# Norm chains with n-wide operands in PSUM, S5 copies of both steps at once, and an order chosen with slack and drawn durations

## The chip, the cores and the metric

The kernel runs on one core of one Trainium2 chip. The core has TensorE (PE, matrix products; PEld is its weight load), VectorE (DVE), ScalarE (ACT), GpSimd (POOL) and SyncE (SP, which issues the DMAs). The metric is the device time of one execution in microseconds (us). Before the change it is 1505.81 us, the median of three runs (1504.4 to 1506.77).

## The reference

It computes two transformer blocks in float32 on 512 tokens of width 1024. Block 1 is an RMS norm, a projection to an attention mixer of three branches (compressed, selected, windowed) and a retention mixer, an output projection, a second RMS norm and a squared-ReLU FFN of width 4096. Block 2 is modulated by a conditioning vector (adaLN): a standardized input goes through a hybrid mixer of an mLSTM (4 heads) and an S5 state space model (32 groups of 16 channels, 64 states), then through a gated FFN with a short convolution, each followed by a layer norm of the scaled residual. What the change touches, cut to the core:

```python
def rms_norm(x, w):
    y = x * lax.rsqrt(jnp.mean(x * x, axis=-1, keepdims=True) + EPS)
    return y * w

def _standardize(x):
    mu = jnp.mean(x, axis=-1, keepdims=True)
    var = jnp.mean(jnp.square(x - mu), axis=-1, keepdims=True)
    return (x - mu) * lax.rsqrt(var + LN_EPS)

# mLSTM, one chunk: numerator, normalizer and the norm of each head
h = num / jnp.maximum(jnp.abs(den), jnp.exp(-m_t))[..., None]
hm = _standardize(hm)

# S5: a diagonal complex recurrence per group, then the output map
_, _, xr, xi = lax.associative_scan(combine, (a_r, a_i, bu_r, bu_i), axis=1)
y = jnp.einsum('gcp,bsgp->bsgc', c_re, xr) - jnp.einsum('gcp,bsgp->bsgc', c_im, xi)
ys = jax.nn.gelu(y + d * u)
```

## The kernel before, in words

All activations lie with channels on the 128 partitions and the 512 tokens along the row. Every large product is a sum of three matmuls: weights and activations are split into a high and a low part (`w`/`xsh`/`xsl`, `wkh`/`wkl` and the like), accumulated in a PSUM bank `ps_g`. Weights arrive by DMA as `wraw`; ACT makes the high part, DVE the low one. PE works on these products nearly all the time, and the norms, the attention, the mLSTM and S5 are threaded into that stream.

The order is not the order of the source. The class `Order` (from line 176) records every instruction with its operands; `add` finds dependences by comparing regions, where `region` (218) takes any PSUM access for the whole bank. `time` (249), `shares` (290) and `latency` (303) are a model of durations, of the port that DVE and POOL share, and of hand-over times. `flush` (311) tries several priorities, plays each through `simulate` (381), which issues per engine what is ready and looks `AHEAD` = 800 instructions ahead, and keeps the order whose modelled end is earliest. `issue` (515) then emits the instructions in that order, so nearly every row of the profile has line 519, and instructions are told apart by their tiles. The order is final: each engine works its own list from first to last, waiting at its head.

The norms need 1/sqrt. `newton` (702) computes it on DVE without a table: a first guess `y` from the bits of `v`, half of `-v` in `a`, three rounds of Newton's method. For up to four columns (one per 128 tokens) each step is done one column at a time, 128x1, with the column as a per-partition scalar. The tile names carry the caller's prefix: `r1`, `rk`, `rq`, `r3` (RMS and retention norms; `r3v`, `r3a`, `r3t`, `r3y`), `rm` (the mLSTM's norm; its inputs `md`, `me`, its result applied to `nm`), `rl` (standardization). The result `..y` is broadcast over the partitions by a PE transpose (`ps_t<-cf,rly`, where `cf` is the identity), which is where PE can wait for DVE.

`standardize` (1315) is used twice, in two halves of 256 tokens each: `add_up` (1306) sums the eight tiles `x` of the residual into two tiles `lsum` (on POOL and DVE in turn) and their squares `sq` (ACT) likewise, for k = 2 to 5; `token_means` (738) then adds the two sums and the tiles of k = 6 and 7 over the channels by tiny matmuls (`ps_s<-lsum,mean`, `ps_s<-x,mean`, `ps_s<-sq,mean`), copies the result (`tm`) and transposes it. `standardize2` (1402) standardizes twice in a row (the output of block 1 and the input of block 2 in one) from six sums per token in `wa`: `wm` and `wv` are its second mean and variance, `wm`, `wa` and `rly` are transposed by PE.

The end of the kernel is the last product of the FFN (`ps_g<-fmh,wkh` ...), whose eight output tiles go in two halves of tokens through `standardize`, then `pair` (product with the factor, then gain and bias on ACT or DVE), then to DRAM. The first half's `pair` work runs beside the second half's matmuls, the second half's behind them.

`s5_out` (2183) makes S5's output in four quarters of groups. Per quarter: 8 matmuls `ps_o<-U,s5k` on the input, and 8 matmuls `ps_o<-s5z,wraw` on the states `X`, which DVE first copies into `s5z`, a tile that is zeroed by POOL and filled by 32 copies of 64 partitions x 32 numbers. Then ACT copies the result to `y5`, and after a way through DRAM a gelu follows. The mLSTM runs beside it (`qkh`, `W`, `Wh`, `nm`; its gate `om` is made by ACT with a bias `gb` that DVE computes).

Of the kernel before, what the change touches and what calls it, by code (L numbers as in the profile page):

```python
# [20 lines left out]
S = 512  # L21
D = 1024
SLOTS = 70
AHEAD = 800
# [151 lines left out]
class Order:  # L176
# [40 lines left out]
    @staticmethod  # L217
    def region(ap, t):

        if t.psum:  # L220
            return 0, 128, 0, 1
        dims, o = [(int(s), int(c)) for s, c in ap.ap], int(ap.offset)
        p0, pc = 0, 1
        if not t.dram:
            (ps, pc), dims = dims[0], dims[1:]
            p0, o = divmod(o, ps)
        lo = o + sum(s * (c - 1) for s, c in dims if s < 0)
        hi = o + sum(s * (c - 1) for s, c in dims if s > 0)
        return p0, p0 + pc, lo, hi + 1

    def add(self, engine, fn, args, kw):
        i, deps, use = len(self.ops), set(), {}
        for a, w in [(a, n == 0) for n, a in enumerate(args)] + [(a, k == "accum_out") for k, a in kw.items()]:
# [4 lines left out]
            r, keep = self.region(a, t), []  # L238
# [10 lines left out]
    def time(self, engine, fn, args, kw):  # L249
# [5 lines left out]
        cols = sum(self.width(a) == 1 for a in aps[1:]) if wide > 1 else 0  # L255
# [9 lines left out]
        if engine == "vector":  # L265
            return 68 + wide * (6.25 if fn == "reciprocal" else 1.042) + 61 * cols + 60 * ("accum_out" in kw)
# [23 lines left out]
    def shares(self, op):  # L290

        aps = [a for a in [*op.args[1:], *op.kw.values()] if hasattr(a, "tensor")]
        if op.engine == "gpsimd":
            return len(aps) > 0
        if op.engine != "vector" or any(a.tensor.name in self.psum for a in [op.args[0], *aps]):
            return False
        one = self.width(op.args[0]) == 1
        return op.fn in ("tensor_tensor", "scalar_tensor_tensor") or op.fn in ("tensor_scalar", "tensor_copy") and not one
# [12 lines left out]
    def flush(self):  # L311
# [11 lines left out]

        best, early, late = None, [0.0] * N, self.latest()
# [56 lines left out]
    def simulate(self, prio, early, alike=0, apart=150.0):  # L381
# [19 lines left out]
        parked, order, events, over = {}, [], [], {}  # L401
        issued, later, low = [op.engine == "sync" for op in ops], [], 0
# [27 lines left out]
        while len(order) < N:  # L430
            now, e = min(((st.free[e] if ready[e] else max(st.free[e], avail[e][0][0]), e)
                          for e in self.ENGINES if ready[e] or avail[e]), default=(math.inf, None))
            if events and events[0][0] <= now:
                time, name = heapq.heappop(events)
                st.live[tiles[name].key].discard(name)
                wake(tiles[name].key, time)
# [23 lines left out]
            else:  # L460
                start[i] = now
                for name in new:
                    wake(tiles[name].key, now)
                if e == "sync":
# [3 lines left out]
                    st.dma = max(now + hold + 650.0, st.dma, lane) + op.time  # L468
# [44 lines left out]
        return SimpleNamespace(order=order, start=start, end=max(fin))  # L513
# [8 lines left out]
class Kern:  # L522
# [167 lines left out]
    def rsqrt(self, ssum, n, scale, eps, name, post=None, bufs=2):  # L690

        v = self.small(name + "v", n, bufs)
# [9 lines left out]
    def newton(self, v, n, name, post=None, bufs=2):  # L702

        V = self.nc.vector
        y, a, t = (self.small(name + c, n, bufs) for c in "yat")
        if n <= 4:

            y_, a_, t_, v_ = ([x[:, j:j + 1] for j in range(n)] for x in (y, a, t, v))
            for j in range(n):
                V.tensor_scalar(y_[j].bitcast(I32), v_[j].bitcast(I32), -0.5, float(0x5F3759DF), op0=OP.mult, op1=OP.add)  # L710
                V.tensor_scalar(a_[j], v_[j], -0.5, None, op0=OP.mult)
            for i in range(3):
                for j in range(n):
# [3 lines left out]
            if post:  # L717
                for j in range(n):
                    V.tensor_scalar(y_[j], y_[j], post, None, op0=OP.mult)
            return y  # L720
        V.tensor_scalar(y.bitcast(I32), v.bitcast(I32), -0.5, float(0x5F3759DF), op0=OP.mult, op1=OP.add)
        V.tensor_scalar(a, v, -0.5, None, op0=OP.mult)
        for _ in range(3):
            V.tensor_tensor(t, y, y, op=OP.mult)
            V.tensor_tensor(t, t, a, op=OP.mult)
            V.scalar_tensor_tensor(y, t, 1.5, y, op0=OP.add, op1=OP.mult)
        if post:
            V.tensor_scalar(y, y, post, None, op0=OP.mult)
        return y
# [8 lines left out]
    def token_means(self, groups):  # L738
# [9 lines left out]
        T.transpose(pt[:, 0:128], t, self.ident)  # L748
        return pt[:, 0:128].rearrange("p (q r) -> p q r", r=32)[:, :, 0]
# [169 lines left out]
    def head_factors(self, st, name):  # L919

        V, A, T = self.nc.vector, self.nc.scalar, self.nc.tensor
        n = st.n

# [209 lines left out]
    def attention(self):  # L1133
# [3 lines left out]
        den = self.const.tile([128, 4, 2, 2, 4], F32, name="den")  # L1137
# [4 lines left out]
        def scores(r, br, i, P):  # L1142
# [6 lines left out]
            for g in range(2):  # L1149
# [9 lines left out]
                A.activation(P[g][:, o], ps[:, 0:n], AF.Exp, bias=mx, accum_out=den[:, i, br, g, r:r + 1])  # L1159
            d = den[:, i, br, :, r]  # L1160
# [145 lines left out]
    def add_up(self, sums, x, k, c):  # L1306
        s, q = sums
        e = (self.nc.gpsimd, self.nc.vector)[k % 2]
        if 1 < k < 6:
            e.tensor_tensor(s[k % 2][:, c], (x[k - 2] if k < 4 else s[k % 2])[:, c], x[k][:, c], op=OP.add)  # L1310
        self.nc.scalar.activation(q[k][:, c], x[k][:, c], AF.Square)
        if 1 < k < 6:
            e.tensor_tensor(q[k % 2][:, c], q[k % 2][:, c], q[k][:, c], op=OP.add)

    def standardize(self, x, hf, sums, each, eps=1e-5):
# [6 lines left out]
        pv = self.token_means([[u[:, tok[j]] for u in t] for t in ([*s, *x[6:]], [*q[0:2], *q[6:]]) for j in range(2)])  # L1322
        m, w, v = (self.small("l" + n, 2, 2) for n in "mwv")
        V.tensor_copy(m, pv[:, 0:2])
        V.scalar_tensor_tensor(w, pv[:, 0:2], -1.0, m, op0=OP.mult, op1=OP.mult)
        if isinstance(eps, float):
            V.scalar_tensor_tensor(v, pv[:, 2:4], eps, w, op0=OP.add, op1=OP.add)
        else:
            V.tensor_tensor(v, pv[:, 2:4], w, op=OP.add)
            for j in range(2):  # L1330
                V.tensor_scalar(v[:, j:j + 1], v[:, j:j + 1], eps[:, 2 * hf + j:2 * hf + j + 1], None, op0=OP.add)
# [70 lines left out]
    def standardize2(self, x, hf, st, gain, bias, each):  # L1402
# [8 lines left out]
        a = self.small("wa", 12, 2).rearrange("p (n j) -> p n j", j=2)  # L1411
        V.tensor_copy(a, pv[:, 0:12].rearrange("p (j n) -> p n j", j=2))
        m, s1, s2, s3, q, q2 = (a[:, n] for n in range(6))
        c1, c2, c3, c4 = (st.cs[:, n:n + 1] for n in range(4))
        v = self.small("wv", 2, 2)
        each_ = lambda *vs: [[u[:, j:j + 1] for u in vs] for j in range(2)]
        for m_, v_, q_ in each_(m, v, q):
            V.tensor_scalar(v_, m_, m_, -1.0, op0=OP.mult, op1=OP.mult)
        for m_, v_, q_ in each_(m, v, q):
            V.tensor_scalar(v_, v_, 1e-5, q_, op0=OP.add, op1=OP.add)  # L1420
# [3 lines left out]
        r = self.newton(v, 2, "rl")  # L1424

        for m_, a1, a2, a3, p_ in each_(m, s1, s2, s3, q2):
            V.tensor_scalar(a1, m_, c1, a1, op0=OP.mult, op1=OP.subtract)
            V.tensor_scalar(a3, m_, c3, a3, op0=OP.mult, op1=OP.subtract)
            V.tensor_scalar(a2, m_, c2, a2, op0=OP.mult, op1=OP.subtract)
            V.tensor_scalar(p_, a2, m_, p_, op0=OP.mult, op1=OP.add)  # L1430
            V.tensor_scalar(p_, a1, a1, p_, op0=OP.mult, op1=OP.subtract)
# [7 lines left out]
        m2, v2 = self.small("wm", 2, 2), self.small("wv", 2, 2)  # L1439
        for v_, p_, r_, a3 in each_(v2, q2, r, s3):  # L1440
            V.tensor_scalar(v_, p_, r_, a3, op0=OP.mult, op1=OP.add)
        for v_, r_ in each_(v2, r):
# [888 lines left out]
```

## Time and profile before

| | |
|---|---|
| median of three runs | 1505.81 us (1504.4 to 1506.77) |
| the profiled execution: its own time | 1505.45 us |
| its span | 1503.3 us |
| granted TensorE clock, mean | 0.991 |
| PE busy | 1461.9 us (97%) |
| DVE / ACT / POOL busy | 1124.8 / 688.6 / 569.8 us |
| on the chain that ended last | PE 86%, DVE 10%, DMA 2%, ACT 1% |

The span runs from the first to the last instruction of the execution; its own time is 2.2 us longer. Busy time of the helpers says little here: with PE busy for 97% of the span, what matters is the few places in which PE is not. Those are read from its waits (what released PE after idling), from the timeline around them, and from the granted clock in windows, since PE can work at less than full clock after it has stood still. Most matmuls show as two records, and ends overlap the next start, so the step from start to start is the time that a matmul costs.

### The profile page before, as it was taken

Reading aid. Unit: us, or ns where it says so; the run is one execution under the profiler, and the core shown is the slowest. Engines: PE = TensorE matmul, PEld = TensorE weight load, DVE = VectorE, ACT = ScalarE, POOL = GpSimd, SP = SyncE. Lnnn points to the kernel's source line nnn. Section 1 sums busy time; section 2 is a strip of 40 time slices with the busy share of each in tenths; the row PEclk is TensorE's granted clock in tenths of the full one; section 3 lists DMA queues with packets and bytes.
Section 4 is the critical chain, followed back from the end, with each engine's and each line's share of the span. In section 5 each row is a group of like instructions: output and inputs, shape, how many; then the busy total and the mean of one; then the engine's idle time right before and its main releaser. Section 6 shows DMA issues by size and latency. Waiting matters only on the chain.

```text
span 1503.3 us, 24351 instructions
## 1 busy us (share of the span) xinstructions
PE 1461.9 (97%) x8738; PEld 1221.4 (81%) x8738; DVE 1124.8 (75%) x2641; ACT 688.6 (46%) x1397; POOL 569.8 (38%) x583
## 2 busy tenths in 40 slices
PE   9999999999999999999999899999999999999996
PEld 6779656888888777899778777878888899998996
DVE  6896798998974674565887863656488999897886
ACT  6454465444333333453563354434265555454553
POOL 6332334240060660143186102120127357464635
PEclk9999999999999999999999899999999999999998
DMA  6731114858731533415313543345311133323331
GB/s 218 224 108 64 56 43 160 267 193 279 235 116 42 176 129 119 153 46 176 107 57 100 158 137 124 119 147 180 143 63 51 50 106 99 116 88 106 100 97 57
DMA packets 81065, 188.34 MB, mean 125 GB/s; under 512 B 18352, under 2 KB 28528, under 8 KB 80944
## 3 DMA queue, kind: packets, MB, share of 16 engines
q1 hardware_dynamic: 80944, 186.78, 38.5%
q8 instruction: 69, 1.13, 0.3%
q14 instruction: 52, 0.43, 0.1%
HBM read 168.70 MB, written 15.17 MB: 122 GB/s over the span
## 4 chain that ended last, share of the span: by engine, by line
PE 86%; DVE 10%; DMA 2%; ACT 1%; issue 1%; POOL 0%; SPq 0%; ACTq 0%; DVEq 0%; POOLq 0%
PE ps_g L519 72%; PE ps_s L519 6%; PE ps_o L519 5%; PE ps_t L519 3%; DVE s5z L519 1%; DVE w L519 1%; DVE x L519 1%; DVE rlt L519 1%; DMA wraw<-in_w_fg_dram 1%; DVE rly L519 0%; DVE r3t L519 0%; DVE rmt L519 0%; DMA wraw<-in_w_f_dram 0%; DVE r3y L519 0%; DMA wraw<-in_w_down_dram 0%
## 5 line engine op out<-in xcount | busy, mean ns | idle before, releaser
L519 DVE TENSOR_TENSOR w<-wraw,w 128x512 fp32r<-128x512 f32 (+2 forms) x390 | 321.3, 837 | 92.2 <-ACT w L519 87.8
L519 ACT ACTIVATE w<-wraw 128x512 fp32r<-128x512 f32 (+1 forms) x398 | 240.3, 609 | 318.0 <-PE ps_g L519 248.6
L519 PE MATMUL ps_g<-xsh,w 128*128 128x256 f32 (+1 forms) x1088 | 278.8, 338 | 2.6 <-DVE w L519 2.2
L519 PE MATMUL ps_g<-xh,w 128*128 128x512 f32 x736 | 240.2, 398 | 0.0
L519 PEld LDWEIGHTS ps_g<-xsh,w 128*128 128x128 f32 x1088 | 188.6, 190 | 28.7 <-DVE w L519 2.6
L519 PE MATMUL ps_g<-xsl,w 128*128 128x256 f32 (+1 forms) x544 | 182.6, 336 | 0.0
L519 PEld LDWEIGHTS ps_g<-xh,w 128*128 128x128 f32 x736 | 137.7, 188 | 33.6 <-issue 1.9
L519 PE MATMUL ps_g<-xl,w 128*128 128x512 f32 x368 | 145.9, 397 | 0.0
L519 PE MATMUL ps_g<-mdh,w 128*128 128x512 f32 (+1 forms) x480 | 143.7, 374 | 0.1
L519 POOL TENSOR_TENSOR x<-x,lc 128x256 f32<-128x256 f32 x72 | 52.6, 773 | 185.9 <-ACT lc L519 173.7
L519 PEld LDWEIGHTS ps_g<-xsl,w 128*128 128x128 f32 x544 | 103.3, 190 | 11.0
L519 PE MATMUL ps_g<-tfh,w 128*128 128x256 f32 x576 | 107.5, 281 | 0.9 <-DVE wo L519 0.4
L519 PEld LDWEIGHTS ps_g<-mdh,w 128*128 128x128 f32 x480 | 87.1, 188 | 17.9 <-issue 0.8
L519 PE MATMUL ps_g<-fmh,w 128*128 128x512 f32 (+1 forms) x332 | 101.4, 375 | 0.0
L519 PEld LDWEIGHTS ps_g<-tfh,w 128*128 128x128 f32 x576 | 89.7, 188 | 2.1 <-DVE wo L519 0.9
L519 PE MATMUL ps_g<-mdl,w 128*128 128x512 f32 (+1 forms) x240 | 89.6, 373 | 0.0
L519 PEld LDWEIGHTS ps_g<-xl,w 128*128 128x128 f32 x368 | 69.2, 188 | 15.6
L519 PE MATMUL ps_g<-tfl,w 128*128 128x256 f32 x288 | 78.0, 281 | 0.0
L519 POOL TENSOR_TENSOR ws<-wraw 128x512 f32<-128x512 f32 x36 | 57.1, 1591 | 51.7 <-DMA wraw<-in_w_fv_dram 27.2
L519 DVE SCALAR_TENSOR_TENSOR raw<-raw,silu 128x1024 f32<-128x1024 f32 x48 | 62.7, 1305 | 9.7 <-DMA raw<-in_w_ada_dram 9.2
L519 PEld LDWEIGHTS ps_g<-fmh,w 128*128 128x128 f32 x332 | 59.8, 188 | 10.3 <-issue 0.2
L519 DVE TENSOR_TENSOR w<-ws,w 128x512 fp32r<-128x512 f32 x72 | 58.7, 829 | 11.1 <-ACT w L519 10.8
(510 smaller groups left out, 3471.1 us busy)
## 6 DMA issues: line engine op xcount, KB each, us to landing
raw<-in_w_ada_dram SPq DMA_DIRECT2D x48, 512.0 KB, 4.3
wraw<-in_w_dram SPq DMA_DIRECT2D x36, 512.0 KB, 3.7
wraw<-in_w_up_dram SPq DMA_DIRECT2D x32, 512.0 KB, 4.2
wraw<-in_w_down_dram SPq DMA_DIRECT2D x32, 512.0 KB, 3.7
wraw<-in_w_fv_dram SPq DMA_DIRECT2D x22, 512.0 KB, 3.9
wraw<-in_w_fg_dram SPq DMA_DIRECT2D x22, 512.0 KB, 3.7
wraw<-in_w_f_dram SPq DMA_DIRECT2D x14, 512.0 KB, 4.3
wraw<-in_w_fd_dram SPq DMA_DIRECT2D x16, 384.0 KB, 3.1
```

What stands on the lines that cost most here:

```text
L519: getattr(getattr(self.nc, op.engine), op.fn)(*op.args, **op.kw)
```

## The change

Five things change; all of it goes through the planner again, so nearly every instruction may stand elsewhere.

1. The planner. Tried durations of all engines but PE are stretched by 1 to 3% and each hand-over by 20 or 40 ns; it looks 2000 instructions ahead; PSUM regions are exact for all engines but PE; each candidate order is replayed twice with drawn durations (`again`), and the lowest mean is kept.
2. `newton` and what feeds it: each step is one instruction over all n columns; `y` and `v` lie in a free part of a PSUM bank (`room`), `a` and `t` in SBUF.
3. `add_up` also sums k = 6 and 7, so `token_means` adds two tiles in place of four; `standardize2` works on both columns at once with PSUM operands.
4. The mLSTM's `md` is made per tile from PSUM.
5. `s5z` is laid out so that one copy moves 64 x 64 numbers: 64 copies in place of 128; the matmuls read `U` with a step of 8 numbers and `s5z` in runs of 8.

```diff
-AHEAD = 800
+TIMES, SPREAD = 2, 0.1
+SLACK = ((1.02, 20.0), (1.01, 40.0), (1.03, 40.0))
+AHEAD = 2000
...
-    def region(ap, t):
-
-        if t.psum:
-            return 0, 128, 0, 1
+    def region(ap, t, bank=True):
+
+        if t.psum and bank:
+            return 0, 128, 0, S
...
-            r, keep = self.region(a, t), []
+            r, keep = self.region(a, t, engine == "tensor"), []
...
-        for prio in [list(range(N))] * 2 + [[late[i] / 1000 + w * i for i in range(N)] for w in (0.2, 0.4, 0.8, 1.2, 2.0, 4.0)]:
-            r = min((self.simulate(prio, early, n) for n in (0, 400, 1500)), key=lambda r: r.end)
-            if best is None or r.end < best.end:
-                best = r
+        todo = [(list(range(N)), SLACK[0])] * 2 + [([late[i] / 1000 + w * i for i in range(N)], k) for w in (0.2, 0.4, 0.8, 1.2) for k in SLACK]
+        for prio, slack in todo:
+            rs = [self.simulate(prio, early, slack, n) for n in (400, 1500)]
+            for r in rs:
+
+                r.score = sum(self.again(r, seed) for seed in range(TIMES)) / TIMES
+                if best is None or r.score < best.score:
+                    best = r
...
-                    time = op.time
+                    time = op.time * (slack[0] if e != "tensor" else 1.0)
...
-                    at[j] = max(at[j], fin[i] + self.latency(op, ops[j]))
+                    at[j] = max(at[j], fin[i] + self.latency(op, ops[j]) + slack[1] * (e != "tensor"))
...
+    def again(self, r, seed):
...
+        vary = (1.0 + SPREAD * R.rand(N) ** 4).tolist()
+        late = (80.0 * R.rand(N)).tolist()
...
     def newton(self, v, n, name, post=None, bufs=2):
 
         V = self.nc.vector
-        y, a, t = (self.small(name + c, n, bufs) for c in "yat")
-        if n <= 4:
-
-            y_, a_, t_, v_ = ([x[:, j:j + 1] for j in range(n)] for x in (y, a, t, v))
-            for j in range(n):
-                V.tensor_scalar(y_[j].bitcast(I32), v_[j].bitcast(I32), -0.5, float(0x5F3759DF), op0=OP.mult, op1=OP.add)
-                V.tensor_scalar(a_[j], v_[j], -0.5, None, op0=OP.mult)
-            for i in range(3):
-                for j in range(n):
-                    V.tensor_scalar(t_[j], y_[j], y_[j], a_[j], op0=OP.mult, op1=OP.mult)
-                for j in range(n):
-                    V.tensor_scalar(y_[j], t_[j], 1.5, y_[j], op0=OP.add, op1=OP.mult)
...
+        out, a, t = (self.small(name + c, n, bufs) for c in "yat")
+        y = self.room[:, 0:n]
         V.tensor_scalar(y.bitcast(I32), v.bitcast(I32), -0.5, float(0x5F3759DF), op0=OP.mult, op1=OP.add)
         V.tensor_scalar(a, v, -0.5, None, op0=OP.mult)
...
+        for i in range(3):
+            V.tensor_tensor(t, a, y, op=OP.mult)
+            V.tensor_tensor(t, t, y, op=OP.mult)
+            V.scalar_tensor_tensor(out if i == 2 and not post else y, t, 1.5, y, op0=OP.add, op1=OP.mult)
...
     def add_up(self, sums, x, k, c):
...
-        if 1 < k < 6:
+        if k > 1:
             e.tensor_tensor(s[k % 2][:, c], (x[k - 2] if k < 4 else s[k % 2])[:, c], x[k][:, c], op=OP.add)
         self.nc.scalar.activation(q[k][:, c], x[k][:, c], AF.Square)
-        if 1 < k < 6:
+        if k > 1:
             e.tensor_tensor(q[k % 2][:, c], q[k % 2][:, c], q[k][:, c], op=OP.add)
...
-        pv = self.token_means([[u[:, tok[j]] for u in t] for t in ([*s, *x[6:]], [*q[0:2], *q[6:]]) for j in range(2)])
+        pv = self.token_means([[t[i][:, tok[j]] for i in range(2)] for t in (s, q) for j in range(2)])
...
-        r = self.newton(v, 2, "rl")
-
-        for m_, a1, a2, a3, p_ in each_(m, s1, s2, s3, q2):
-            V.tensor_scalar(a1, m_, c1, a1, op0=OP.mult, op1=OP.subtract)
...
+        r = self.newton(self.room[:, 2:4], 2, "rl")
+
+        V.scalar_tensor_tensor(s1, m, c1, s1, op0=OP.mult, op1=OP.subtract)
...
-                T.matmul(o, kk[g], self.U[q][:, g, :], start=g == 0, stop=False, skip_group_check=True)
+                T.matmul(o, kk[g], self.U[q][:, g, :].rearrange("p (s j) -> p j s", j=8), start=g == 0, stop=False, skip_group_check=True)
             for i in range(2):
-                x = self.t2("s5z", F32, (128, 4, 2, 64))
-                G.memset(x, 0.0)
+
+                x = self.t2("s5z", F32, (128, 2, 8, 4, 8))
                 for e in range(2):
                     r = slice(64 * e, 64 * e + 64)
+                    G.memset(x[r, 1 - e], 0.0)
                     for n in range(4):
-                        for j in range(2):
-                            V.tensor_copy(x.rearrange("p g e (s j) -> p j e g s", j=8)[r, 2 * n + j, e],
-                                          self.X[n][r, j, :, i, 4 * q:4 * q + 4].rearrange("p s g -> p g s"))
+                        V.tensor_copy(x[r, e, 2 * n:2 * n + 2], self.X[n][r, :, :, i, 4 * q:4 * q + 4].rearrange("p j s g -> p j g s"))
                 for g in range(4):
-                    T.matmul(ps[:, 128 * g:128 * g + 128], m[:, i, g, :], x[:, g].rearrange("p e k -> p (e k)"),
+                    T.matmul(ps[:, 128 * g:128 * g + 128], m[:, i, g, :], x[:, :, :, g, :],
                              start=False, stop=i == 1, skip_group_check=True)
```

Three places show how the order moves. The first is PE in the second half of `standardize2`, from the transposes of `wa` (the mean) to those of `rly` (the factor), both of which DVE makes; the `ps_g` rows are matmuls of the mixer's input projection (`xsh`, `xsl` the split input). Before:

```order
L519 MATMUL ps_t<-cf,wa 128x128 x2
L519 MATMUL ps_g<-xsl,w 128x256
L519 MATMUL ps_g<-xsh,w 128x256 x2
L519 MATMUL ps_g<-xsl,w 128x256
L519 MATMUL ps_g<-xsh,w 128x256 x2
L519 MATMUL ps_g<-xsl,w 128x256
L519 MATMUL ps_g<-xsh,w 128x256 x2
L519 MATMUL ps_g<-xsl,w 128x256
L519 MATMUL ps_g<-xsh,w 128x256 x2
L519 MATMUL ps_g<-xsl,w 128x256
L519 MATMUL ps_g<-xsh,w 128x256
L519 MATMUL ps_t<-cf,rly 128x128 x2
```

Changed; the transposes of `wa` stand 27 rows above the first row shown here, with nothing but matmuls `ps_g<-xsh,w` and `ps_g<-xsl,w` between:

```order
L597 MATMUL ps_g<-xsh,w 128x256
L597 MATMUL ps_g<-xsh,wkh 128x256
L597 MATMUL ps_g<-xsl,wkh 128x256
L597 MATMUL ps_g<-xsh,wkl 128x256
L597 MATMUL ps_g<-xsh,wkh 128x256
L597 MATMUL ps_g<-xsl,wkh 128x256
L597 MATMUL ps_g<-xsh,wkl 128x256
L597 MATMUL ps_g<-xsh,wkh 128x256
L597 MATMUL ps_g<-xsl,wkh 128x256
L597 MATMUL ps_g<-xsh,wkl 128x256
L597 MATMUL ps_t<-cf,rly 128x128 x2
```

Between `wa` and `rly` 14 matmuls stood before; now there are 49.

The second place is DVE around the mLSTM's norm and the S5 copies: `nm` is the mLSTM's output being normed, `s5z` and `X` are S5's, `gb` is the bias that ACT needs for the gate `om`. Before:

```order
L519 TENSOR_SCALAR rmt<-rmy,rma 128x1 x4
L519 TENSOR_SCALAR rmy<-rmt,rmy 128x1 x4
L519 TENSOR_SCALAR nm<-nm,mv,rmy 128x256 x4
L519 COPY s5z<-X 64x4x8 x58
L519 TENSOR_SCALAR gb<-nw_899 128x1
L519 COPY s5z<-X 64x4x8 x2
L519 SCALAR_TENSOR_TENSOR om<-om,ps_t 128x512
```

Changed; `rma`, `rmt` and the PSUM operands `ps_t` are the norm chain of `nm`:

```order
L597 TENSOR_SCALAR gb<-nw_894 128x1
L597 TENSOR_TENSOR rmt<-rmt,ps_t 128x4
L597 SCALAR_TENSOR_TENSOR ps_t<-rmt,ps_t 128x4
L597 TENSOR_TENSOR rmt<-rma,ps_t 128x4
L597 TENSOR_TENSOR rmt<-rmt,ps_t 128x4
L597 SCALAR_TENSOR_TENSOR ps_t<-rmt,ps_t 128x4
L597 TENSOR_TENSOR rmt<-rma,ps_t 128x4
L597 TENSOR_TENSOR rmt<-rmt,ps_t 128x4
L597 SCALAR_TENSOR_TENSOR rmy<-rmt,ps_t 128x4
L597 TENSOR_SCALAR nm<-nm,mv,rmy 128x256 x4
L597 COPY s5z<-X 64x64 x32
L597 SCALAR_TENSOR_TENSOR om<-om,ps_t 128x512 x2
```

`gb` stood behind the norm and 58 copies, with two more copies between it and `om`; it now stands within the norm chain, the last 32 of the (wider) copies follow, and `om` comes after them.

The third place is ACT at the end: `sq` are the squares of the second half's output tiles (which the last means wait for), `pair` the first half's last step, `lc` belongs to the last norm. Before:

```order
L519 ACTIVATE sq<-x_2142 128x256
L519 ACTIVATE sq<-x_2143 128x256
L519 ACTIVATE pair<-pair,nw_899 128x256 x5
L519 ACTIVATE sq<-x_2144 128x256
L519 ACTIVATE pair<-pair,nw_899 128x256
L519 ACTIVATE sq<-x_2145 128x256
L519 ACTIVATE pair<-pair,nw_899 128x256 x2
L519 ACTIVATE sq<-x_2146 128x256
L519 ACTIVATE sq<-x_2147 128x256
L519 ACTIVATE sq<-x_2148 128x256
L519 ACTIVATE lc<-ps_t 128x256
L519 ACTIVATE pair<-pair,nw_899 128x256 x6
```

Changed:

```order
L597 ACTIVATE sq<-x_2136 128x256
L597 ACTIVATE sq<-x_2137 128x256
L597 ACTIVATE sq<-x_2138 128x256
L597 ACTIVATE sq<-x_2139 128x256
L597 ACTIVATE pair<-pair,nw_894 128x256 x8
L597 ACTIVATE sq<-x_2140 128x256
L597 ACTIVATE sq<-x_2141 128x256
L597 ACTIVATE lc<-ps_t 128x256
L597 ACTIVATE pair<-pair,nw_894 128x256 x6
```

The first half's `pair` stood in three lots among the squares, with three squares behind the last lot; now all eight stand in one lot, and two squares come after it.

## Rows read from the trace of the kernel before

**Rows 1.** The page: its head, and busy time with share and instructions by engine.

```profile
span 1503.3 us, 24351 instructions
...
PE 1461.9 (97%) x8738; PEld 1221.4 (81%) x8738; DVE 1124.8 (75%) x2641; ACT 688.6 (46%) x1397; POOL 569.8 (38%) x583
```

**Rows 2.** Waits of PE over the span (total us, times, longest us).

```profile
PE ps_t L519 <- DVE rly L519: 10.7, 8, 3.5
PE ps_t L519 <- DVE nm L519: 5.1, 3, 2.4
PE ps_o L519 <- ACT om L519: 4.2, 1, 4.2
PE ps_g L519 <- DVE w L519: 2.5, 3, 1.8
PE ps_t L519 <- DVE r3y L519: 1.6, 2, 1.1
```

**Rows 3.** Windows, 840 to 850: length; PE, PEld, DVE, ACT, POOL busy; PEclk, DMA, GB/s.

```profile
840.00:850.00 10.00, 5.82 (x33) 4.86 (x32) 9.48 (x48) 3.29 (x6) 0.07 (x1) 0.73 0.24 80
```

**Rows 4.** Timeline of PE in S5: start, duration, instruction, count, wait before it.

```profile
839.33 2.00 PE L519 MATMUL ps_o<-s5z,wraw 128*128 128x128 f32 x16
...
847.30 3.68 PE L519 MATMUL ps_o<-U,s5k 128*128 128x64 f32 x16 [4.18 <-ACT om L519]
...
850.76 3.73 PE L519 MATMUL ps_o<-s5z,wraw 128*128 128x128 f32 x16
...
856.32 1.95 PE L519 MATMUL ps_o<-U,s5k 128*128 128x64 f32 x16
```

**Rows 5.** Timeline of DVE, then ACT, in the same stretch.

```profile
836.05 10.24 DVE L519 COPY s5z<-X 64x32 f32<-64x32 f32 x58
846.30 0.15 DVE L519 TENSOR_SCALAR gb<-nw 128x1 f32<-128x1 f32 x1
...
846.56 0.69 ACT L519 ACTIVATE om<-ps_g,gb 128x512 f32<-128x512 f32 x1 [8.63 <-DVE gb L519]
```

**Rows 6.** Timeline of the tail: PE, then ACT, then DVE.

```profile
1489.94 0.41 PE L519 MATMUL ps_s<-sq,mean 128*32 128x128 f32 x4
...
1495.26 0.69 PE L519 MATMUL ps_t<-cf,rly 128*128 128x128 f32 x2 [3.50 <-DVE rly L519]
...
1485.61 1.10 ACT L519 ACTIVATE pair<-pair,nw 128x256 f32<-128x256 f32 x2 [0.42 <-DVE pair L519]
...
1489.47 0.42 ACT L519 ACTIVATE sq<-x 128x256 f32<-128x256 f32 x1 [1.35 <-DVE x L519]
...
1496.51 3.06 ACT L519 ACTIVATE pair<-pair,nw 128x256 f32<-128x256 f32 x6 [4.27 <-DVE pair L519]
...
1487.60 0.42 DVE L519 TENSOR_TENSOR sq<-sq 128x256 f32<-128x256 f32 x1
```

**Rows 7.** Timeline of DVE: a norm chain of four columns, its begin and what follows it.

```profile
976.85 0.16 DVE L519 SCALAR_TENSOR_TENSOR me<-md,mv 128x4 f32<-128x4 f32 x1
977.05 0.17 DVE L519 TENSOR_SCALAR rmv<-me 128x4 f32<-128x4 f32 x1
...
981.38 1.38 DVE L519 TENSOR_SCALAR nm<-nm,mv,rmy 128x256 f32<-128x256 f32 x4
```

**Rows 8.** Timeline of PE in the second half of the second standardization.

```profile
1131.61 0.38 PE L519 MATMUL ps_t<-cf,wa 128*128 128x128 f32 x2
...
1135.16 0.62 PE L519 MATMUL ps_t<-cf,rly 128*128 128x128 f32 x2 [1.54 <-DVE rly L519]
```

**Rows 9.** Timeline of PE: the first of the last means, and the one 24 records later.

```profile
1488.85 0.30 PE L519 MATMUL ps_s<-lsum,mean 128*32 128x128 f32 x2
...
1489.53 0.39 PE L519 MATMUL ps_s<-x,mean 128*32 128x128 f32 x4
```

**Rows 10.** Timeline of ACT: a table load and the activation behind it.

```profile
871.32 1.28 ACT L519 ACT_TABLE_LOAD   x1
872.62 0.63 ACT L519 ACTIVATE y<-y 128x512 f32<-128x512 f32 x1
```

More of the change, by code (lines that the diff above doesn't have):

```diff
@@ L253, in time @@
         wide = max(self.width(a) for a in aps)
-        cols = sum(self.width(a) == 1 for a in aps[1:]) if wide > 1 else 0
+        cols = sum(self.width(a) == 1 for a in aps[1:]) if wide > 1 else sum(hasattr(a, "tensor") for a in (
+            args[2:4] if fn == "tensor_scalar" else args[2:3] if fn == "scalar_tensor_tensor" else kw.values()))
         if engine == "tensor":
@@ L265, in time @@
         if engine == "vector":
+            if fn == "tensor_scalar" and not any(a.tensor.name in self.psum for a in aps) and aps[1].dtype == F32:
+                return 68 + 0.52 * wide + 61 * cols
             return 68 + wide * (6.25 if fn == "reciprocal" else 1.042) + 61 * cols + 60 * ("accum_out" in kw)
@@ L294, in shares @@
             return len(aps) > 0
-        if op.engine != "vector" or any(a.tensor.name in self.psum for a in [op.args[0], *aps]):
+        if op.engine != "vector" or any(a.tensor.name in self.psum for a in aps):
             return False
-        one = self.width(op.args[0]) == 1
-        return op.fn in ("tensor_tensor", "scalar_tensor_tensor") or op.fn in ("tensor_scalar", "tensor_copy") and not one
+        return op.fn in ("tensor_tensor", "scalar_tensor_tensor") or op.fn in ("tensor_scalar", "tensor_copy") and op.args[0].tensor.name not in self.psum
     LATENCY = {"tensor": dict(tensor=0, scalar=197, vector=197), "scalar": dict(tensor=227, scalar=143, vector=142, gpsimd=180),
@@ L401, in simulate @@
         parked, order, events, over = {}, [], [], {}
+        count, gone, slots = {}, {}, {}
         issued, later, low = [op.engine == "sync" for op in ops], [], 0
@@ L435, in simulate @@
                 st.live[tiles[name].key].discard(name)
+                gone.setdefault(tiles[name].key, []).append(name)
                 wake(tiles[name].key, time)
@@ L462, in simulate @@
                 for name in new:
-                    wake(tiles[name].key, now)
+                    key = tiles[name].key
+                    count[key] = count.get(key, 0) + 1
+                    if count[key] > tiles[name].cap:
+                        slots[name] = gone[key][count[key] - tiles[name].cap - 1]
+                    wake(key, now)
                 if e == "sync":
@@ L467, in simulate @@
                     lane = min(st.lanes)
-                    st.dma = max(now + hold + 650.0, st.dma, lane) + op.time
+                    st.dma = max(now + hold + 650.0, st.dma, lane) + op.time * slack[0]
                     fin[i] = st.dma + 900.0
@@ L1438, in standardize2 @@
         rb = self.columns(r)
[L1439 to L1442, printed above, removed]
[L1443 to L1448 removed]
+        m2, v2, w2 = self.small("wm", 2, 2), self.small("wv", 2, 2), pv[:, 272:274]
+        self.room = pv[:, 288:512]
+        V.scalar_tensor_tensor(m2, s1, -1.0, r, op0=OP.mult, op1=OP.mult)
+        V.tensor_tensor(v2, q2, r, op=OP.mult)
+        V.tensor_tensor(w2, v2, s3, op=OP.subtract)
+        V.tensor_tensor(v2, w2, r, op=OP.mult)
+        V.tensor_scalar(w2, v2, c4, None, op0=OP.add)
+        r2 = self.newton(w2, 2, "rl")
         mb = self.columns(m2)
```

145 lines of the change are left out of this document (97 added, 48 removed).

## The prediction, made before the changed kernel was run

> **What bounds the kernel now.** I read the page's busy line first. TensorE (PE) is busy for 1461.9 of 1503.3 us, so only 41.4 us of the span are not matmul time, and everything that the change can win without fewer matmuls lies in there or in the clock [rows 1]. The last matmul row ends at 1495.95 (1495.26 + 0.69), so 7.35 us of the 41.4 are the tail after it and 34.0 us are gaps between matmuls [rows 6].
>
> Next I read PE's waits. The reader is to see that few names make up these gaps: `rly` 10.7 us in eight waits (3.5 of it in the tail), `nm` 5.1 in three, `om` 4.2 in one, `r3y` 1.6 in two [rows 2]. `rly`, `r3y` and `nm` are the ends of one routine, the 1/sqrt of the norms, which VectorE (DVE) does on numbers of 1 column. `om` belongs to the S5 stage. `w`, 2.5 us in three, is a wait for weights that DVE prepares; no part of the change is aimed at it, so I leave it in (0 to -2.5 if the new order places them better).
>
> Then I looked at the clock by windows of 10 us, since an idle PE can be paid for twice. In 840 to 850 the granted clock is 0.73 [rows 3]. The row behind the `om` wait shows what that means: 16 records `ps_o<-U,s5k` take 3.68 us right after 4.18 us of idling, and the same 16 take 1.95 us at 856.32. So PE fell to the lower of its levels (1.2 GHz) during the wait. The 16 `s5z` records behind it take 3.73, those at 839.33 take 2.00 [rows 4].
>
> **The norm chains.** A chain for four columns begins with `rmv` at 977.05 and is done when `nm` starts at 981.38: 4.3 us [rows 7]. It is 32 instructions of 128x1, four for each step. Afterwards it is 11 instructions that each take all columns and depend on one another (two to set up, three rounds of three). What such a step costs is shown by `me` and `rmv`, 128x4 and dependent: 0.20 us from start to start [rows 7]. 11 x 0.20 = 2.2 us, so 2.1 us less per chain [rows 7]. That the operands now lie in PSUM is not shown for this very chain. At best it costs nothing; at worst I take double (0.40 a step), which would make the chain as long as before. I take the 0.20, the nearest row. For two columns the gain is smaller, between 0 and 1.4 us, since the old chain had 16 instructions; I use 0.8.
>
> The order does the other half. In the second standardization, PE issues `wa`'s transposes at 1131.61, works until 1133.62, and then stands 1.54 us for `rly` [rows 8]. Between the two stood 14 matmuls, now 49: at the same rate the cover grows from 2.0 us to some 6 or 7, over a chain of about 3.5 us. By the same count (matmuls between a norm's trigger and its use) the cover grows at every `r3y` (an estimate: from some 4 to 6 us to 9 or more) and at most `rly` (by 0.2 to 4 us). For `nm` it stays about as it is, and there the shorter chain must do it: the longest of these waits is 2.4 us, against 2.1 saved. So I take away `rly` 7.2 (10.7 less the tail's 3.5), `r3y` 1.6 and `nm` 5.0: **-13.8 us**.
>
> What is late next is the work ahead of these chains, and other engines. DVE stays the busiest helper, and the longer look ahead keeps more of its work queued. An order that is made anew makes small waits of its own; I allow one seventh of the 13.8: **+2 us**.
>
> **S5.** At 836.05 DVE starts 58 copies into `s5z` in a row, 10.24 us (0.176 each); `gb`, one small instruction, stands behind them at 846.30, ACT's `om` behind `gb` at 846.56 after 8.63 us of idling, and PE behind `om` [rows 5]. In the new order `gb` stands inside the norm chain, ahead of the last 32 copies. There are 64 copies of twice the width. If width costs nothing they take 11.3 us in place of 22.5; if time went by elements, 22.5 as before. I take the middle, 0.26 each, so 16.9, which is 5.6 us less on DVE. The wait for `om` then hangs on nothing long: **-4.2 us** (bounds 0 and -4.2). The clock comes back with it: 3.68 - 1.95 and 3.73 - 2.00 are **-3.5 us** (bounds 0 and -3.5).
>
> **Means.** Each of the four calls of the first standardization loses 8 of 16 tiny matmuls. 24 records (12 matmuls) lie between 1488.85 and 1489.53, so 8 matmuls are 0.45 us: 4 x 0.45 = **-1.8 us** [rows 9]. The two extra sums for k=6 and 7 go to DVE and POOL, which hides them except in the tail.
>
> **Tail.** The last big matmul is over at 1488.85, the last means start at 1489.94, 1.1 us later [rows 6, 9]. In the new order ACT has eight `pair` activations of 0.55 (1.10 for two) ahead of the last two `sq`, and the `rly` transposes that release those pairs stand only 29 matmuls before the end of the last product, about 3.4 us (rows 8 give at most 0.14 for one, transposes included; I take 0.12). Pairs then end about -3.4 + 1.3 + 8 x 0.51 = 2.0 us after it (1.3 is 1496.51 less 1495.26, 0.51 the step of `pair` x6), the two `sq` 0.8 later (0.42 each), and the new sum over `sq` needs 0.4 more (the 0.42 of such a sum on DVE): 3.2 in place of 1.1, +2.1, and less 0.8 for the chain: **+1.3 us** (0 to +4) [rows 6].
>
> **ACT.** The order holds two more table loads, around the gelu of S5. The row shows 1.28 us for one, and the next activation starts at 872.62, 0.03 us after its end [rows 10]. So 2.6 us more on ACT, which was busy for 3.29 of 10 us here [rows 3]: between 0 and 2.6 on the path; I take **+1.0**.
> The Trainium skill ("ScalarE: Activation LUTs", What ACT_TABLE_LOAD costs) adds a drain of about 1.38 us to a load of about 1.28 us; the load agrees with the row, the drain does not show in it. By the page the two would be an estimated 5.3 us on ACT, and the sum at most 2.7 higher.
>
> **The sum.** -13.8 + 2 - 4.2 - 3.5 - 1.8 + 1.3 + 1.0 = -19.0 from the profiled execution's 1505.45 (which is 0.4 below the median shown) gives 1486.
>
> **Rivals.**
> *Half of it.* S5 is cured, but DVE's queue sets the norms' ends, not the chain's length; half of the norm waits stay while the rest goes as forecast. For it: DVE is busy for 75% of the span, and its other work stands between the steps of a chain [rows 1]. Against it: in the stretch of rows 7 the 32 instructions fill the 4.3 us alone, 0.135 each, so there the chain's length is what counts. -6.9 + 2 - 4.2 - 3.5 - 1.8 + 2.3 = -12.1, so 1493.
> *It does not do what it says.* The new order keeps its covers on paper, and the waits come back under other names at as many places. For it: the old order was also one whose waits were meant to be covered, and the trace has 34 us of them. Then only the means and part of `om` are won: -1.8 - 4.2 + 2.3 = -3.7, 1502.
> *Strided reads of the matmuls.* `U` is read with a step of 8 numbers, `s5z` in runs of 8. No row of before shows a strided moving operand. 16 `U` records of 64 columns take 1.95 us and 16 `s5z` records of 128 columns 2.00, so columns are not what sets `U`'s time, and a read of half the speed could be hidden [rows 4]. There are four such groups of 16: doubling costs 4 x 1.95 = 7.8 us, 1494. From 3.4 times (0.42 us a record) the whole gain is gone, and at five times it is +31, so 1517: slower than before.
> The Trainium skill ("SBUF — State Buffer", Door 1: The DMA port swizzle) says that SBUF is read in lines of 16 bytes and that every access which crosses to a new line pays, so four fp32 numbers are the widest free step. By that rule `U` pays for every number and `s5z` does not; the page gives no size, and no run here shows one yet. It is the reason why this rival has any chance.
>
> **How the numbers follow.** Forecast 1486 (own range 1476 to 1495): 0.62. Half of it 1493 (1489 to 1499): 0.22. Waits return 1502 (1497 to 1508): 0.10. Strided reads at five times 1517: 0.06. A measurement of this kernel can tell about 0.2%, 3 us, from no change. Faster by more: 0.62 + 0.22 + 0.04 of the third + 0.01 of the fourth = 0.89. Within: 0.05 of the third. Slower: 0.01 + 0.05 = 0.06. The low end of the range takes all gaps but the tail's 3.5, the clock and the means, with none of the costs: 30.5 + 3.5 + 1.8 = 35.8, so 1470, and I leave 1 us for the first loads, which no order hides: 1471. The high end reaches through the second case to 1499.
>
> **What would show it.** PE's waits for `rly`, `r3y` and `nm` should add up to under 4 us outside the tail; a `newton` of four columns should take 2.2 us, 0.20 a step with PSUM operands (0.40 would be the bound failing). The wait for `om` at S5 should be gone and the window around it show a clock of 0.95 or more. `U` records should keep 0.12 us; 0.24 or more says the third rival. The rest between the last big matmul and the span's end should be 1 to 3 us longer. I am wrong if PE's gaps outside tail and start still hold over 15 us, or if the busy time of PE grew.

## The result, and the profile after

The changed kernel took 1483.84 us (median of four runs, 1482.84 to 1485.38), against 1505.13 for the kernel before; the ratio is 0.9858, 95% interval 0.9841 to 0.9875. The forecast was 1486, its range 1471 to 1499. The profiled execution, the quickest of the four, has a span of 1481.1 us, 22.2 less than before. Head and busy line of its page:

```profile
span 1481.1 us, 23939 instructions
...
PE 1453.2 (98%) x8674; PEld 1218.3 (82%) x8674; DVE 1076.7 (73%) x2332; ACT 694.2 (47%) x1401; POOL 577.4 (39%) x599
```

The 22.2 us fall into two parts. PE is busy 8.7 us less (1461.9 to 1453.2, [rows 1]); idle time before matmuls fell from 34.0 to 20.5 us, and the tail after the last matmul stayed at 7.4. PE's largest waits, and that for `sq` (total us, times, longest):

```profile
PE ps_t L597 <- DVE rly L597: 4.7, 3, 3.2
PE ps_g L597 <- ACT wo L597: 1.8, 2, 1.0
PE ps_s L597 <- POOL lsum L597: 1.3, 1, 1.3
PE ps_g L597 <- POOL w L597: 1.3, 1, 1.3
PE ps_o L597 <- issue: 1.3, 1, 1.3
PE ps_g L597 <- DVE w L597: 1.2, 4, 0.4
...
PE ps_s L597 <- POOL sq L597: 1.0, 1, 1.0
```

Against [rows 2]: `nm`, `om` and `r3y` are gone from the list, `rly` fell from 10.7 to 4.7, of which 3.2 is the tail. Waits at other places grew by about 3 us, 2.3 of them in the tail (`lsum`, `sq`).

A norm chain of four columns, the row that answers to [rows 7], on DVE:

```profile
958.65 0.17 DVE L597 TENSOR_SCALAR ps_t<-ps_t 128x4 int32<-128x4 int32 x1
958.86 0.16 DVE L597 TENSOR_SCALAR rma<-ps_t 128x4 f32<-128x4 f32 x1
959.05 0.16 DVE L597 TENSOR_TENSOR rmt<-rma,ps_t 128x4 f32<-128x4 f32 x1
...
960.61 0.16 DVE L597 SCALAR_TENSOR_TENSOR rmy<-rmt,ps_t 128x4 f32<-128x4 f32 x1
```

From the first guess (958.65) to the start of the last step (960.61) are ten steps in 1.96 us, 0.196 each; the chain takes 2.1 us. The 4.3 before, counted from `rmv`, hold one step of 0.20 more. The second standardization, answering to [rows 8]; PE, then DVE:

```profile
1109.45 0.38 PE L597 MATMUL ps_t<-cf,wa 128*128 128x128 f32 x2
...
1116.76 0.43 PE L597 MATMUL ps_t<-cf,rly 128*128 128x128 f32 x2 [1.14 <-DVE rly L597]
```

```profile
1114.70 0.16 DVE L597 TENSOR_TENSOR rlt<-rlt,ps_t 128x2 f32<-128x2 f32 x1
1116.22 0.42 DVE L597 TENSOR_TENSOR fy<-fy,ps_g 128x256 f32<-128x256 f32 x1 [1.36 <-ACT fy L597]
1116.56 0.15 DVE L597 SCALAR_TENSOR_TENSOR rly<-rlt,ps_t 128x2 f32<-128x2 f32 x1
```

7 us lie between the two transposes now, and PE still waited 1.14 us, since the last step of the chain stood behind an op (`fy`) that itself waited 1.36 us for ACT. The S5 stretch, answering to [rows 3] to [rows 5]: the window, then PE, then DVE:

```profile
840.00:850.00 10.00, 10.00 (x70) 8.97 (x70) 4.58 (x11) 9.96 (x17) 3.19 (x4) 1.00 0.62 193
```

```profile
824.37 2.06 PE L597 MATMUL ps_o<-U,s5k 128*128 128x64 f32 x16
826.26 1.07 PE L597 MATMUL ps_o<-s5z,wraw 128*128 128x128 f32 x8
828.61 1.13 PE L597 MATMUL ps_o<-s5z,wraw 128*128 128x128 f32 x8 [1.28 <-issue]
```

```profile
824.20 1.38 DVE L597 TENSOR_SCALAR nm<-nm,mv,rmy 128x256 f32<-128x256 f32 x4
825.52 2.64 DVE L597 COPY s5z<-X 64x64 f32<-64x64 f32 x16
```

The clock is 1.00, 16 `U` records take 2.06 us, and sixteen copies of twice the width take 2.64 us, 0.165 each (0.16 to 0.19 in the other lots): they cost about what the narrow ones did. A wait of 1.28 us is left before `s5z`; the profile names only issue there. The likely cause is the sixteen copies, done at 828.16: in mended, below, they stand earlier, and that wait is gone. The tail, answering to [rows 6] and [rows 9]; PE, then ACT:

```profile
1464.32 0.28 PE L597 MATMUL ps_g<-fmh,wkl 128*128 128x256 f32 x1
1465.94 0.41 PE L597 MATMUL ps_s<-lsum,mean 128*32 128x128 f32 x4 [1.34 <-POOL lsum L597]
...
1467.60 0.41 PE L597 MATMUL ps_s<-sq,mean 128*32 128x128 f32 x4
...
1472.97 0.69 PE L597 MATMUL ps_t<-cf,rly 128*128 128x128 f32 x2 [3.15 <-DVE rly L597]
```

```profile
1462.05 4.04 ACT L597 ACTIVATE pair<-pair,nw 128x256 f32<-128x256 f32 x8
1466.00 0.70 ACT L597 ACTIVATE sq<-x 128x256 f32<-128x256 f32 x2
```

From the end of the last big matmul (1464.44, its start and a step of 0.12) to the end of the span are 16.7 us, 14.45 before. The last means start 3.2 us after that matmul (1467.60), 1.1 before; from them to the transposes of `rly` are 5.37 us, 5.32 before.

### The profile page after: what moved, and what is told of

It reads as the page before. It is cut to its first block, busy times and chain, and to the rows that moved or that the text cites. A ratio compares the mean times of both kernels' runs of the same rounds, so it can differ in the third digit from the quotient of the medians.

```text
span 1481.1 us, 23939 instructions
## 1 busy us (share of the span) xinstructions
PE 1453.2 (98%) x8674; PEld 1218.3 (82%) x8674; DVE 1076.7 (73%) x2332; ACT 694.2 (47%) x1401; POOL 577.4 (39%) x599
## 5 line engine op out<-in xcount | busy, mean ns | idle before, releaser
L597 DVE TENSOR_TENSOR w<-wraw,w 128x512 fp32r<-128x512 f32 (+2 forms) x390 | 316.7, 824 | 123.4 <-ACT w L597 121.6
L597 ACT ACTIVATE w<-ws 128x512 fp32r<-128x512 f32 x72 | 45.3, 630 | 44.2 <-PE ps_g L597 33.8
```

Source lines behind the costliest of these rows:

```text
L597: getattr(getattr(self.nc, op.engine), op.fn)(*op.args, **op.kw)
```

## The experiments

After the result there were three accounts of it. A: shorter chains and longer covers share the gain, as forecast. B: the new order makes it. C: the edits of the norm chains and the S5 copies make it, whichever planner orders them. Four kernels set one against the other.

**planner_only.** Before's kernel code with `class Order` of the changed kernel, prices of instructions included (its second-best candidate order).

```diff
...
-        self.issue(best)
+        self.issue(sorted(runs, key=lambda r: r.score)[1])
```

> The kernel code of before (old norm chains, four-tile means, 128 small S5 copies) with the changed planner; the planner's second-best candidate order is issued. Theory A (chains and covers share the gain): about 1494 us, the r3y and om waits gone since the order covers them, but nm and a good part of the rly waits left (4 us or more outside the tail). Theory B (the order alone makes the gain): 1487 us or less, PE's gaps outside the tail about as few as in the changed kernel, some 15 us. Theory C (the shorter chains and copies make it): 1500 us or more, since the same long chains meet a new order.

1520.62 us, ratio 1.0111 (1.0087 to 1.0135): slower than before. Its waits of PE:

```profile
PE ps_t L596 <- DVE rly L596: 10.5, 3, 6.2
PE ps_g L596 <- DVE w L596: 6.2, 4, 3.1
PE ps_o L596 <- DVE s5z L596: 5.0, 5, 1.5
```

The new planner gives the long chains far more cover at some places (57 matmuls from `wa` to `rly` at the place of [rows 8], 14 before) and none at another (0 from `wm` to the next `rly`), and PE waits there and elsewhere. B falls; old_norms, below, has the long chains in this planner's best order.

**edits_only.** The changed code with before's `class Order` and its reach.

```diff
-AHEAD = 2000
+AHEAD = 800
...
```

> The changed kernel code (norm chains in PSUM, two-tile means, 64 wide S5 copies) with the planner of before, which treats every access to a PSUM bank as one to the whole bank. Theory A: about 1494 us, nm gone or under 1 us, rly about halved, other waits as before. Theory B: 1500 us or more, the waits come back at other places. Theory C: 1487 us or less.

1483.58 us, ratio 0.9863 (0.9844 to 0.9883), the same as the changed kernel. Its largest waits:

```profile
PE ps_t L519 <- DVE rly L519: 4.2, 3, 3.4
PE ps_g L519 <- DVE w L519: 3.4, 2, 3.2
```

`nm` and `r3y` are not in the list. And the covers grew here as well: 41 matmuls from `wa` to `rly` at the place of [rows 8], by the planner of before. So with short chains the planner of before makes longer covers too. C.

**old_norms.** The changed kernel with `rsqrt`, `newton`, `standardize2` and `mlstm_head` of before.

> The changed kernel with the norm chains of before (rsqrt, newton, the second standardization and the mLSTM's md as they were, 128x1 at a time), all else as changed, ordered by the changed planner. Theory A: about 1490 us, 6 us slower than the changed kernel, with nm and rly waits back at 4 us or more outside the tail. Theory B: within 3 us of the changed kernel's 1484, since the planner finds covers for the long chains as well. Theory C: 1495 us or more.

1509.51 us, ratio 1.0042 (1.0029 to 1.0054): without the new chains, everything is lost and more.

**old_s5.** The changed kernel with `s5_out` of before.

> The changed kernel with the S5 output stage of before (128 copies of 64x32, U read with unit step), ordered by the changed planner. Theory A: about 1487 us, with one wait of 2 to 4 us in the S5 stretch for s5z or om. Theory B: within 2 us of the changed kernel, since the order moves gb ahead of the copies all the same. Theory C: 1489 us or more, with the om wait and the lower clock back.

1492.71 us, ratio 0.9923 (0.9903 to 0.9943): 0.65% slower than the changed kernel. The time is as C said, and the lower clock is back (0.81 and 0.85 in the windows at 840 and 850), but not the `om` wait: PE's longest there is one of 3.5 us for `W`.

The next four ask how much of it is luck of an order, and what in the chains does it.

**norms_only.** The kernel of before with the new chains alone.

> The kernel of before, its own planner, with the new norm chains alone (rsqrt, newton, both standardizations' algebra, the mLSTM's md); the four-tile means and the old S5 copies stay. Theory C, now ahead after the first four runs (the shorter chains make most of the gain, whichever planner orders them): 1488 to 1493 us, waits for r3y and nm gone, rly under 1.5 us outside the tail, the om wait in S5 still there or turned into an s5z wait. Rival D (the parts only work together, or the four first runs were mostly the luck of one order): 1497 us or more.

1484.82 us, ratio 0.9869 (0.9854 to 0.9884). The chains alone give nearly all, more than theory C had said. `om` is not among its waits although the S5 copies are the old ones:

```profile
PE ps_g L519 <- DVE w L519: 4.6, 1, 4.6
PE ps_t L519 <- DVE rly L519: 4.2, 3, 3.4
PE ps_t L519 <- DVE nm L519: 3.1, 1, 3.1
```

An `nm` wait of 3.1 us stayed, at 825.6 in the S5 stretch, and with it the lower clock (0.84 and 0.65 in the windows at 820 and 830).

**edits_old_s5.** All edits but the S5 stage, planner of before.

> All edits of the kernel code but the S5 stage, with the planner of before. Theory C: the S5 copies are worth about what they were under the changed planner (8.9 us), so 1491 to 1494, with DVE waits in the S5 stretch. Rival D: within 3 us of 1483.6 (the planner of before finds an order that hides the 128 copies too), in which case the 8.9 us were a matter of that one order.

1488.33 us, ratio 0.9898 (0.9878 to 0.9917), between the two expectations. The S5 edit is worth 0.65% under the one planner, 0.35% under the other (where the two intervals just overlap), and next to nothing by norms_only against edits_only (0.9869, 0.9863): its worth hangs on the order around it.

**sbuf_chains.** Every engine's instructions in the changed kernel's order; only where `room` lies is changed, with `y`, `v` and the few other operands of the chains in it.

```diff
...
+    def sroom(self):
+        return self.small("room", 128, 4)
...
-        self.room = pt[:, 256:512]
+        self.room = self.sroom()
...
```

> The changed kernel, every engine's instructions in exactly the same order, but the part of a PSUM bank in which the norm chains keep y and v (room) is a tile in SBUF. Rival P (the PSUM operands themselves matter: in SBUF a two-tensor step of DVE meets POOL's use of the shared port): steps grow from 0.19 to 0.25 us or more where POOL works, the rly and nm waits come back, 1486 us or more. Theory N (only the number of instructions and their dependence matter): within 2 us of the changed kernel, steps at 0.18 to 0.20 us.

1501.0 us, ratio 0.9971 (0.9959 to 0.9983): four fifths of the gain are gone with the same instructions in the same order. PE's waits for `rly` are 13.7 us, and its gaps before the last matmul are 33.2 us, nearly those of before. The last chain on DVE, beside POOL's four subtractions:

```profile
1489.09 0.43 DVE L571 SCALAR_TENSOR_TENSOR room<-rlt,room 128x2 f32<-128x2 f32 x1
1489.44 0.41 DVE L571 TENSOR_TENSOR x<-x,ps_t 128x256 f32<-128x256 f32 x1
1489.78 0.43 DVE L571 TENSOR_TENSOR rlt<-rla,room 128x2 f32<-128x2 f32 x1
1490.24 0.16 DVE L571 TENSOR_TENSOR rlt<-rlt,room 128x2 f32<-128x2 f32 x1
1490.43 0.16 DVE L571 SCALAR_TENSOR_TENSOR room<-rlt,room 128x2 f32<-128x2 f32 x1
```

```profile
1487.42 2.77 POOL L571 TENSOR_TENSOR x<-x,lc 128x256 f32<-128x256 f32 x4 [3.33 <-ACT lc L571]
```

While POOL works (to 1490.19) each small step takes 0.43 us; the next ones, with nothing else changed, take 0.16. The same steps in the changed kernel, also beside POOL's four subtractions (1470.32 to 1473.09):

```profile
1470.61 0.15 DVE L597 TENSOR_TENSOR rlt<-rla,ps_t 128x2 f32<-128x2 f32 x1
...
1471.01 0.15 DVE L597 TENSOR_TENSOR rlt<-rlt,ps_t 128x2 f32<-128x2 f32 x1
...
1471.40 0.16 DVE L597 SCALAR_TENSOR_TENSOR ps_t<-rlt,ps_t 128x2 f32<-128x2 f32 x1
```

With one operand in PSUM they take 0.15. The Trainium skill ("SBUF — State Buffer", Who interferes with whom) states that a VectorE instruction with two SBUF inputs contends with a GpSimd instruction that reads SBUF, and that one with at most one SBUF input does not, outside the two-port modes of VectorE; these rows agree, 0.43 against 0.15 us. The old form of the chain, one column at a time, did not meet that collision. In the kernel before, all 48 instructions of one of its two kinds lie between 258 and 274 ns, with POOL busy or not (ns: least, median, most):

```profile
L519 DVE TENSOR_SCALAR rlt<-rly,rla x48: 258/265/274, 655.3 to 1494.8; 128x1 f32<-128x1 f32 x48
```

But it took 32 instructions in place of 11 for four columns. The order here is one planned for chains with PSUM operands; what a new order would win back for chains in SBUF was not tried.

**after_second.** The second-best candidate order of the changed kernel.

```diff
...
-        self.issue(best)
+        self.issue(sorted(runs, key=lambda r: r.score)[1])
```

> The changed kernel, but the second-best candidate of the planner is issued in place of the best. If one candidate is about as good as another: within 3 us of 1483.8. If the choice among candidates carries the result (rival D): 1490 us or more.

1485.52 us, ratio 0.9876 (0.9861 to 0.9891): within 2 us.

The last four look at a rival, at the waits that were left, and at the candidates of before.

**unit_u.** `U` read with unit step, the order of instructions unchanged. It leaves out the reordering of the tokens that the output needs.

```diff
-                T.matmul(o, kk[g], self.U[q][:, g, :].rearrange("p (s j) -> p j s", j=8), start=g == 0, stop=False, skip_group_check=True)
+                T.matmul(o, kk[g], self.U[q][:, g, :], start=g == 0, stop=False, skip_group_check=True)
```

> The changed kernel in exactly its order, but the matmuls on U read it with unit step (so the tokens of a group stand in another order, and the output with them). The rival of strided reads: each 16 records, 2.06 to 2.09 us in the changed kernel, fall back to 1.95 us, and the whole falls by more than that. Theory N (the step costs next to nothing): 16 records at 1.95 to 2.05 us, the whole within 1 us of 1483.8.

1484.83 us, ratio 0.9851 (0.9836 to 0.9867). One of its groups on PE:

```profile
828.15 1.89 PE L571 MATMUL ps_o<-U,s5k 128*128 128x64 f32 x16
```

1.89 in place of 2.06 us, 0.01 us a record, 0.7 us in all: the step of 8 costs something, and the kernel cannot tell it.

**tail_only.** The order of the changed kernel with the end rearranged by hand: on ACT the last squares (`sq`), on DVE the last sums into `sq` and `lsum`, and on POOL its last two of these stand ahead of the first half's last `pair` work.

```diff
...
-        self.issue(best)
+        self.issue(SimpleNamespace(order=[int(i) for i in ORDER]))
```

> The changed kernel in its order but for the end: DVE makes the last two output tiles and their sums ahead of the first half's last four pairs, ACT squares them as soon as they are there, POOL sums k=6 before its last subtraction for the first half. If the later means are what makes the tail 2 us longer than before: from the end of the last big matmul to the span's end 15.0 to 15.6 us in place of 16.7, and 1482.0 to 1483.0. If the tail is set by something else (the chain and the pairs behind it): within 0.5 us of 1483.8.

1482.72 us, ratio 0.9842 (0.9828 to 0.9857); 16.0 us from the last big matmul to the span's end, 0.6 less. The sums on DVE show why not more:

```profile
1462.99 0.95 DVE L571 TENSOR_TENSOR sq<-sq 128x256 f32<-128x256 f32 x1
...
1465.42 0.94 DVE L571 TENSOR_TENSOR sq<-sq 128x256 f32<-128x256 f32 x1
```

0.95 us, beside POOL's sums and subtractions, for what took 0.42 before with POOL idle [rows 6], and 0.66 and 0.81 at the end of the changed kernel. The interval overlaps that of the changed kernel, so no gain is shown.

**mended.** That end, and five more places: the last `rly` step of the second standardization ahead of `fy`, `rqy` and `ce` likewise ahead of the op before them, two `vt` ops, two `wo` ops of ACT, and four `nm` ops behind the `s5z` copies are moved in the list `ORDER`.

> The changed kernel in its order but for the end as in the run before it and five places where PE still waited for an instruction that stood behind another one's wait: rly and rqy and ce ahead of the op before them on DVE, two vt ahead of xc, two wo on ACT ahead of fmh and tfh, the nm of the mLSTM behind the sixteen s5z copies that PE wants first. If those waits are each the fault of one place in the order: 1476 to 1479, PE's gaps down from 20.5 to about 14 us. If they only move on to the next instruction: 1481 or more.

1482.14 us, ratio 0.9838 (0.9824 to 0.9853). Gaps are 18.6 us in place of 20.5, not 14: the `vt` wait came back as one for `w` (1.2 us), that for `rly` as one for `wm` (1.0), `s5z` as `nm` (0.5). It beats the kernel before; that it beats the changed kernel is not shown.

**before_second.** The second-best candidate order of before's own planner.

```diff
...
-        self.issue(best)
+        self.issue(sorted(runs, key=lambda r: r.end)[1])
```

> The kernel of before with its own planner, issuing its second-best candidate. If one candidate is about as good as another with the old chains too: within 5 us of before's 1505, and the 1520 of the old chains under the changed planner are that planner's. If with long chains the candidates scatter: 1512 or more, or 1498 or less, and the 1520 say little on the planner.

1516.87 us, ratio 1.0067 (1.005 to 1.0084), 10 us above the best (1506.67 in the same runs). With long chains two candidates lie 10 us apart, and the 1520 of planner_only, a second candidate too, don't show the new planner to be worse; with the short ones two lie 2 us apart (after_second). One pair each is little to go by.

## Why the prediction was right

Sign and size were right, 1486 against 1483.84, and most terms stand. In the profiled executions the 22.2 us are 12.4 for the norm waits, 4.2 for `om` and 8.7 of PE's busy time, less 0.9 of new waits and 2.2 in the tail. The sign of being wrong stayed away: of 20.5 us of gaps 6.1 lie in the tail and 3.0 at the start, which leaves 11.4, under the 15. The part on where covers come from does not stand.

- **Norm chains, -13.8.** `rly` lost 5.7 us outside the tail, `r3y` 1.6, `nm` 5.1: 12.4. The step of 0.20 us was right. That it held because the operands are in PSUM I had not seen: I called PSUM a cost that is zero at best, and sbuf_chains shows it to be what makes the wide form pay in this order.
- **"The order does the other half"**: this step failed. The covers did grow, but they grow with before's planner as well (edits_only, norms_only), at the same time. What was new in the planner gave nothing that can be measured.
- **New small waits, +2, and the tail, +1.3.** About 3 us of waits came elsewhere, 2.3 of them in the tail; the tail grew by 2.2 us. The sum is right, the parts are not. The last means came 2.1 us later, as worked out. The 0.8 that the shorter chain was to save there did not come: from the last means to `rly` it is 5.37 us after 5.32. In either order DVE's subtractions of 128x256, 0.41 us each, stand between the steps, and the first steps follow each other by 0.40 us (1470.61, 1471.01, 1471.40 above) in place of 0.20.
- **S5, -4.2 for `om`, and -3.5 for the clock.** `om` is gone, and the two groups of 16 records run at full clock (3.68 to 2.06, 3.73 to 1.97 in the like). The clock term was too small: PE is busy 8.7 us less, of which the means are 1.8 by the forecast, and the windows at 730 and 890, which I left out, are back at 1.00 too. Before, and after them the window at 730 in unit_u:

```profile
730.00:740.00 10.00, 10.00 (x77) 8.16 (x76) 8.08 (x32) 2.58 (x5) 0.00 (x0) 0.83 0.34 107
...
890.00:900.00 10.00, 10.00 (x42) 8.07 (x41) 5.96 (x12) 3.31 (x6) 0.62 (x1) 0.88 0.26 80
```

```profile
888.34 1.42 PE L519 MATMUL ps_t<-cf,nm 128*128 128x128 f32 x4 [2.36 <-DVE nm L519]
```

```profile
730.00:740.00 10.00, 10.00 (x37) 7.19 (x37) 5.98 (x21) 3.32 (x11) 0.77 (x1) 0.66 0.17 55
```

The one at 890 lies behind a wait of 2.36 us for `nm`, so the chains brought it back. The one at 730 is luck: PE did not stand still in it, and unit_u, which up to there runs the changed kernel's instructions in the same order, has 0.66 where the changed kernel has 1.00. What lowers the clock there was not tried apart; just ahead, in all three, stand the small matmuls of `gc`. At 0.83 the window costs some 1.7 us, an estimate (0.17 of 10 us), and that much of the 22.2 is not the change's. The copies took about the lower bound (0.165), not the middle (0.26).
- **ACT, +1.0.** Six loads in place of four, 7.7 us, and no wait of PE behind the four around S5's gelu (839.96 to 886.67), where two stood before: 0. A load that the kernel before had as well now stands ahead of the 1.14 us wait for `rly` of the second standardization:

```profile
1114.48 1.28 ACT L597 ACT_TABLE_LOAD   x1 [3.24 <-DVE ps_t L597]
1115.77 0.42 ACT L597 ACTIVATE fy<-fy 128x256 f32<-128x256 f32 x1
```

DVE's `fy` follows at 1116.22, `rly` at 1116.56, PE's transposes at 1116.76. By these rows at least part of that wait comes from the load, which was not tried apart; I had looked only at S5.
- **Rivals.** Half of it, and that it does not do what it says, did not come. The second, that a new order brings its waits back, is what planner_only and before_second show for long chains. Strided reads cost 0.7 us.

What stays open is why long chains leave the candidates so far apart. The planner of before counted 0.07 us for a 128x1 step that takes 0.18 from start to start, so it took a long chain for half as long as it is; the planner of the change prices such steps near 0.19, and the long chains were no faster for it. That the wrong price made the waits of before is argued, not shown.

## What to carry to other kernels

A chain of tiny dependent VectorE steps that PE waits for should be as few instructions as possible, over all columns at once, and beside a busy GpSimd one of the two inputs should be in PSUM: the same steps took 0.43 us with both in SBUF, 0.15 with one in PSUM. Before giving an order the credit, run the new code under the old planner and a second candidate under each. And when a wait is mended by moving one instruction, look at what stands next: here most of it came back at the neighbour.

## What the hardware showed that I had not expected

VectorE copies of 64 partitions took 0.165 us each with 64 numbers a row (0.16 to 0.19 by lot) and 0.176 with 32, so here the number of copies set the time, and not their width. A moving operand with a step of 8 float32 numbers cost 0.13 us a matmul record against 0.12 with unit step.
